# Hybrid retention and GLA layer: the last gates beside the last attention, two heads' branch products in one PSUM sum, half of the output projection in seven products

## The chip, the core and the metric

The kernel runs on one core of one Trainium2 chip. The metric is the device time of one execution in microseconds, and lower is better. A core has a matrix engine (TensorE, PE in the profile; its weight loads are listed as PEld), a vector engine (VectorE, DVE), a scalar engine (ScalarE, ACT), a general one (GpSimd, POOL) and SyncE (SP), which here only issues transfers. Each engine runs its own list of instructions in order and waits on semaphores. Matrix products are summed in PSUM, which VectorE and ScalarE read; everything else lies in SBUF, and the inputs in DRAM.

## The reference

One layer over 512 positions (and 16 meta positions ahead of them) of width 1024, with two branches that a learned gate merges:

```python
u = rms_norm(h, norm_gain)
proj = u @ w_in          # rq, rk, rv, rg, gq, gk, gv, gg, glr, m_ret, m_gla
o_ret = retention_chunked(rope(rq), rope(rk) * RET_QK_DIM ** -0.5, rv)   # 4 heads
o_ret = head_group_norm(o_ret, ret_norm_gain) * silu(rg)                 # 2048 wide
o_gla = gla_chunked(gq, gk, gv, log_a)
o_gla = head_rms_norm(o_gla, gla_norm_gain) * silu(gg)                   # 1024 wide
merged = sigmoid(m_ret) * (o_ret @ w_branch_ret) + sigmoid(m_gla) * (o_gla @ w_branch_gla)
out = rms_norm(h + merged @ w_out, final_norm_gain)                      # meta rows dropped
```

All inputs are float32.

## The kernel before

Float32 accuracy is had from a split: each operand is written as a high part in the fp32r format and a low part, the rest (`split`, line 155: a ScalarE cast for the high part, a VectorE subtraction for the low). A product then takes three matmuls, high by high, high by low and low by high (`mm3`, line 190).

The kernel is one long stream of such products on TensorE, with the other engines' work set beside it. A "dense" generator makes products and a "chain" generator makes a step of attention or of some other dependent work; `weave` (line 206) takes a step of the chain after each step of the dense one. The order in which the program is written is a wish: the framework's planner simulates the engines and puts on each what is ready first, so an instruction written later can stand earlier. `after` (line 160) fixes one instruction behind another on an engine, `pin` and `order` do this for the dense products, and `act` and `vec` for ScalarE and VectorE at the start.

Most projections use `quad` (line 259): a 512-wide block of the result is made from two column blocks and two row halves by seven products (24 matmuls of 256 columns each) instead of eight. For that, sums of weight blocks are needed (`x3`, `x1` and two running sums) and sums of the activations, which are made once at the start (forms S1 to S4 beside A11, A12, A22). With `adds=True` the weight sums x3 and x1 come from accumulating transfers that POOL issues (line 277); with `adds=False` VectorE makes them (lines 330 and 331). Three PSUM tiles a, b and c hold the results, and ScalarE copies one of them aside before the next product is added onto it (`copy`, line 309). Weights come into six buffers ("raw", line 251), their high and low parts into three each. There are two sets of four PSUM banks: `ppt` and `pat` (lines 149 to 153).

The stages in time are: the start (the first projection, GLA's values of pair 0, is fed block by block, lines 512 to 573, with 11 warm-up matmuls ahead of it at line 541; after it the scaled x is made in place at line 580); GLA's two pairs, with their gates; then the four retention heads. Of a head, `ret_qk`, `ret_g` and `ret_v` are quads, `ret_scores` makes the decayed scores, and `ret_attention` (line 1095) has six steps: four blocks of values with a group norm each (VectorE statistics, a power on POOL at line 203, a scaling on ScalarE), and two steps of transposes that write the split head output `oh`, `ol`. `ret_branch` (line 1177) multiplies a head's output by its 512 rows of `w_branch_ret`: 8 tiles of 128 x 512, 12 matmuls each. Heads 0 to 2 copy each tile out on ScalarE and add it to the DRAM buffer `kept2` by an accumulating transfer (`collect`, line 905). GLA's gated result waits in `kept`, also in DRAM.

At the end, `weave(run(ret_branch(2), gates_ret()), every(ret_attention(3), 2))` at line 1203 runs head 2's branch and the second half of the retention gates (the quad `mr1`) beside head 3's attention. `gates_ret` (line 1149) also loads `kept2` into `kr` (line 1164, on POOL behind the last power), multiplies it by the gates and accumulates `kept` onto it (`part`, lines 1156 to 1160). Head 3's branch (line 1221) is merged tile by tile: gate times PSUM (line 1184), plus `kr` (1185), then split into `mh`, `ml`. The output projection is two halves of 512 columns: `proj_b` (line 404) with its four weights in order, and lines 1250 to 1269 with all four weights at hand, a row block of 128 at a time, the last in two halves of 256. `evac_out` (line 1226) adds the residual, sums squares, and, when a row block is whole, scales and stores it.

Of the kernel before, what the change touches and what calls it, by code (L numbers as in the profile page):

```python
# [108 lines left out]
def hybrid_kernel(ctx: ExitStack, tc: tile.TileContext, I, out: bass.AP):  # L109
# [17 lines left out]

    nc.scalar.activation(pad[:, :1], one, AF.Copy, scale=one)
# [130 lines left out]
    def quad(cols, rows, name, evac, meta=None, adds=True, ahead=False, behind=None):  # L259
# [8 lines left out]

        def block(kh, n):
            return w_in[kh * 512:kh * 512 + 512, cols[n]:cols[n] + 256].rearrange("(k p) c -> p k c", p=P)  # L270
# [22 lines left out]
        def product(i, form, w, ps, fresh, ready=None):  # L293
            hi, lo = ready or prepare(i, w)
            for t in range(2):
                col = slice(t * P, (t + 1) * P)
                for kk in range(4):
                    u = [f[form][:, kk, col] if rows else f[form][:, kk, :256] for f in (fh, fl)]
# [105 lines left out]
    def proj_b(src, col, left, name, evac):  # L404

        pss = [ppt(f"{name}_p{t}") for t in range(NTB)]
# [107 lines left out]
    for q in range(4):  # L514
        raw = wraw(f"gv0_{q}_w", (P, 2, 512))
        for s in (slice(0, 1), slice(1, 2)) if q == 0 else (slice(0, 2),):
            k0, n = 2 * q + s.start, s.stop - s.start
            nc.sync.dma_start(u[k0 // 4][:, k0 % 4:k0 % 4 + n], I["xt"][:, k0:k0 + n])
# [21 lines left out]
    for _ in range(11):  # L540
        nc.tensor.matmul(wps, wzero[:, :P], wzero, start=True, stop=True)
# [10 lines left out]
    pss = [ppt(f"gv0_p{t}") for t in range(NTB)]  # L552
    for q in range(4):
        raw = graw[q]
        hi, lo = wsplit([P, 2, 512], f"gv0_{q}")
        for kk in range(2):
            kh, k = divmod(2 * q + kk, 4)
            g = ng[:, 2 * q + kk:2 * q + kk + 1]
            nc.scalar.activation(xh[kh][:, k, :, :HT], u[kh][:, k], AF.Copy, scale=g)
            nc.vector.scalar_tensor_tensor(xl[kh][:, k, :, :HT], u[kh][:, k], g, xh[kh][:, k, :, :HT].bitcast(F32),  # L560
                                           op0=ALU.mult, op1=ALU.subtract)
            split(hi[:, kk, :], lo[:, kk, :], raw[:, kk, :])
# [532 lines left out]
    def ret_attention(h):  # L1095
# [3 lines left out]
        oh = rp.tile([P, 4, T], F32R, tag="oh", name=f"oh{h}")  # L1099
        ol = rp.tile([P, 4, T], F32R, tag="ol", name=f"ol{h}")  # L1100
# [48 lines left out]
    def gates_ret():  # L1149
# [6 lines left out]
        def part(c, s):  # L1156

            k = kr[c][:, :, s]
            after(nc.vector.tensor_mul(k, k, sigr[c][:, :, s]), low[1])
            nc.gpsimd.dma_start(k, kept[:, 2 * c:2 * c + 2, s], accum_op=ALU.add)  # L1160

        for c in range(KD // 2):
            kr[c] = rp.tile([P, 2, T], F32, tag=("sh", "sl", "cs", "dec")[c], name=f"kr{c}")
            after(nc.gpsimd.dma_start(kr[c], kept2[:, 2 * c:2 * c + 2, :]), R["pow"])
            if c < 2:
                pend.append((4 + c, lambda c=c: part(c, slice(0, T))))
        one = sp.tile([P, 1], F32, tag="one", name="sig1")
        pend.append((3, lambda: after(nc.scalar.activation(one, mhalf, AF.Sigmoid), low[0])))

        def evac(n, th, p, q):  # L1170
            s = slice(th * 256, (th + 1) * 256)
            gate(sigr[2 + n][:, :, s], p, q, th, n)
            pend.append((2, lambda: part(2 + n, s)))

        yield from quad((C_MR + 512, C_MR + 768), False, "mr1", evac, adds=False)

    def ret_branch(h):
        def evac(c, ps):
            t = tmp(f"mt{h}{c}")
            if h < 3:  # L1180
                nc.scalar.copy(t, ps)  # L1181
                collect(kept2[:, c, :], t, h == 0)
            else:
                nc.vector.tensor_mul(t, sigr[c // 2][:, c % 2, :], ps)  # L1184
                nc.vector.tensor_add(t, t, kr[c // 2][:, c % 2, :])
                split(mh[c // 2][:, c % 2, :], ml[c // 2][:, c % 2, :], t)

        oh, ol = R["o", h]
        yield from branch(I["w_branch_ret"], h * 512, oh, ol, f"br{h}", evac, pat if h < 2 else ppt)

    for h in range(4):
# [12 lines left out]
    mh, ml = [[cp.tile([P, 4, T], F32R, tag=f"x{n}0", name=f"m{n}0"),  # L1204
               *[cp.tile([P, 2, T], F32R, tag=f"f{n}{i}", name=f"m{n}{i}") for i in (S2, S3)]] for n in "hl"]
    mh, ml = [[m[0][:, :2], m[0][:, 2:], *m[1:]] for m in (mh, ml)]

    def merged(k, t):
        return [m[k // 2][:, k % 2, t * P:(t + 1) * P] for m in (mh, ml)]


    fgb = rp.tile([P, D], F32, tag="sg", name="fgb")
    nc.sync.dma_start(fgb, I["final_norm_gain"].to_broadcast([P, D]))
    hs = [rp.tile([P, NTB, 512], F32, tag="vh", name="hs0"), rp.tile([P, NTB, 512], F32, tag="vl", name="hs1")]

    def residual():
        for half in range(2):
            nc.sync.dma_start(hs[half], I["x"][:, half * 512:(half + 1) * 512].rearrange("(t p) d -> p t d", p=P))
            yield

    weave(ret_branch(3), residual(), skip=3)
# [4 lines left out]
    def evac_out(half):  # L1226
        def f(t, ps, o=0, n=512):
            hh = hs[half][:, t, o:o + n]
# [71 lines left out]
```

## Time and profile before

| | |
|---|---|
| time, median of 3 runs | 781.37 us (781.2 to 782.45) |
| the profiled execution's own time | 781.41 us |
| its span, first to last instruction | 779.6 us |
| granted TensorE clock, mean | 0.998 |
| instructions | 13602 |
| HBM read, written | 98.15 MB, 15.73 MB |

A row of the page's fifth part or of the groups is one kind of instruction: line, engine, operation, out<-in tiles, shape and count, then busy time in us and mean ns, then the idle time before it and who ended it. A row of the timeline or chain begins with the start and the duration in us. A row of the stretches gives the stretch, its length, and for each engine the busy time and in brackets the number of instructions. TensorE is pipelined: a matmul is listed for longer than it holds the engine, so its price is read from the distance between starts.

### The profile page before, as it was taken

How to read it: one execution, taken by the hardware profiler on the slowest of the kernel's cores; microseconds unless marked ns; L12 is line 12 of the kernel's file. 1: busy time of each engine (PE TensorE's matmuls, PEld its weight loads, DVE VectorE, ACT ScalarE, POOL GpSimd, SP SyncE). 2: the span in 40 equal slices, each digit the busy share in tenths (PEclk: the TensorE clock that was granted, in tenths of full speed). 3: DMA queues.
4: the chain of work that ended last, by engine and by line, in shares of the span. 5: the costliest groups of instructions: out<-in, count | busy, mean ns of one | idle time of the engine just before them, and what ended most of it. 6: DMA issues, size and time to landing. Idle time of an engine off the chain costs nothing.

```text
span 779.6 us, 13602 instructions
## 1 busy us (share of the span) xinstructions
PE 767.5 (98%) x5404; PEld 696.3 (89%) x5404; DVE 571.1 (73%) x824; ACT 450.6 (58%) x745; POOL 138.9 (18%) x190
## 2 busy tenths in 40 slices
PE   9999999999999999999999999999999999999896
PEld 6799989999888899999899999989999998898685
DVE  5868788676654679779967688977687988585832
ACT  8889764678564456545656545646455744363422
POOL 2311120101322312100320100330111101321031
PEclk9999999999999999999999999999999999999999
DMA  9862511833249973833693553694465336698102
GB/s 289 264 154 78 111 55 55 190 110 97 79 124 232 238 160 99 189 108 109 201 252 115 134 137 111 170 246 130 124 158 120 110 108 186 120 328 230 55 5 104
DMA packets 92871, 114.76 MB, mean 147 GB/s; under 512 B 5764, under 2 KB 79364, under 8 KB 92552
## 3 DMA queue, kind: packets, MB, share of 16 engines
q1 hardware_dynamic: 73400, 84.27, 34.4%
q0 software_dynamic: 19264, 29.37, 19.7%
q8 instruction: 42, 0.69, 0.4%
q10 hardware_dynamic: 144, 0.26, 0.1%
q14 instruction: 21, 0.17, 0.1%
HBM read 98.15 MB, written 15.73 MB: 146 GB/s over the span
## 4 chain that ended last, share of the span: by engine, by line
PE 86%; DVE 5%; DMA 3%; ACT 3%; issue 2%; POOL 1%; POOLq 0%; DVEq 0%; ACTq 0%
PE rv_b L303 6%; PE rqk_b L303 6%; PE rg_b L303 6%; PE rqk_c L303 3%; PE gv_p L570 3%; PE rg_c L303 3%; PE mg_b L303 3%; PE rv_c L303 3%; PE br_p L191 3%; PE br_p L195 3%; PE br_p L194 3%; PE gg_b L303 2%; PE bg_p L191 2%; PE bg_p L195 2%; PE bg_p L194 2%
## 5 line engine op out<-in xcount | busy, mean ns | idle before, releaser
L191 PE MATMUL br_p<-oh,br_h 128*128 128x512 f32 x128 | 50.6, 395 | 0.0
L195 PE MATMUL br_p<-oh,br_l 128*128 128x512 f32 x128 | 50.6, 395 | 0.0
L194 PE MATMUL br_p<-ol,br_h 128*128 128x512 f32 x128 | 50.5, 395 | 0.0
L156 ACT CAST rv_h<-rv_w 128x1024 fp32r<-128x1024 f32 x24 | 25.3, 1052 | 29.3 <-DVE rv_w L333 10.1
L907 POOL DMA_DIRECT2D kept<-mt x24 | 20.9, 871 | 110.4 <-ACT mt L1181 110.4
L1117 ACT ACTIVATE on<-av,nm,g_r 128x512 f32<-128x512 f32 x16 | 12.5, 778 | 45.4 <-DVE nm L1115 45.4
L156 DVE TENSOR_TENSOR rv_l<-rv_w,rv_h 128x1024 fp32r<-128x1024 f32 x24 | 29.3, 1223 | 8.8 <-ACT rv_h L156 8.8
L156 DVE TENSOR_TENSOR rg_l<-rg_w,rg_h 128x1024 fp32r<-128x1024 f32 x20 | 24.4, 1220 | 7.9 <-ACT rg_h L156 7.9
L191 PE MATMUL wo_p<-wo_h,mh 128*128 128x512 f32 (+1 forms) x72 | 26.9, 374 | 2.5 <-DVE mt L1184 2.5
L195 PEld LDWEIGHTS br_p<-oh,br_l 128*128 128x128 f32 x128 | 24.0, 188 | 5.8
L194 PEld LDWEIGHTS br_p<-ol,br_h 128*128 128x128 f32 x128 | 24.0, 188 | 5.1
L277 POOL DMA_DIRECT2D rqk_x<-in_w_in_dram x8 | 10.5, 1310 | 101.6 <-DMA rqk_x<-in_w_in_dram 40.5
L156 ACT CAST rg_h<-rg_w 128x1024 fp32r<-128x1024 f32 x20 | 21.1, 1053 | 13.0 <-PE br_p L194 5.0
L191 PEld LDWEIGHTS br_p<-oh,br_h 128*128 128x128 f32 x128 | 24.0, 188 | 5.1
L156 DVE TENSOR_TENSOR rqk_l<-rqk_w,rqk_h 128x1024 fp32r<-128x1024 f32 x20 | 24.4, 1220 | 5.4 <-ACT rqk_h L156 5.4
L156 ACT CAST rqk_h<-rqk_w 128x1024 fp32r<-128x1024 f32 x20 | 21.0, 1049 | 12.4 <-DVE rqk_w L333 6.7
L303 PE MATMUL rqk_b<-fh,rqk_h 128*128 128x256 f32 x96 | 27.0, 282 | 0.0
L303 PE MATMUL rg_b<-rg_h,fl 128*128 128x256 f32 x96 | 27.0, 281 | 0.0
L303 PE MATMUL rv_b<-rv_h,fl 128*128 128x256 f32 x96 | 27.0, 281 | 0.0
L303 PE MATMUL rqk_b<-fh,rqk_l 128*128 128x256 f32 x96 | 27.0, 281 | 0.0
L303 PE MATMUL rv_b<-rv_l,fh 128*128 128x256 f32 x96 | 27.0, 281 | 0.0
L303 PE MATMUL rg_b<-rg_l,fh 128*128 128x256 f32 x96 | 26.9, 281 | 0.0
(647 smaller groups left out, 3166.4 us busy)
## 6 DMA issues: line engine op xcount, KB each, us to landing
rv_w<-in_w_in_dram SPq DMA_DIRECT2D x16, 512.0 KB, 4.1
br_w<-in_w_branch_ret_dram SPq DMA_DIRECT2D x16, 512.0 KB, 3.7
rqk_w<-in_w_in_dram SPq DMA_DIRECT2D x12, 512.0 KB, 4.6
rg_w<-in_w_in_dram SPq DMA_DIRECT2D x12, 512.0 KB, 4.6
kept<-mt POOLq DMA_DIRECT2D x24, 256.0 KB, 5.2
bg_w<-in_w_branch_gla_dram SPq DMA_DIRECT2D x8, 512.0 KB, 3.7
mr_w<-in_w_in_dram SPq DMA_DIRECT2D x8, 512.0 KB, 3.5
kept<-gb POOLq DMA_DIRECT2D x16, 256.0 KB, 4.2
```

The source lines that it names most:

```text
L156: return nc.scalar.copy(hi, src), nc.vector.tensor_sub(lo, src, hi.bitcast(F32))
L191: m = nc.tensor.matmul(o, lh, rh, start=first, stop=False)
L194: nc.tensor.matmul(o, lh, rl, start=False, stop=False)
L195: m = nc.tensor.matmul(o, ll, rh, start=False, stop=last)
L277: x = nc.gpsimd.dma_start(t, block(0, 1), accum_op=ALU.add)
L303: m = nc.tensor.matmul(ps[:, t, :], l, r, start=first and j == 0, stop=kk == 3 and j == 2, skip_group_check=not fresh or t == 1)
L570: m = nc.tensor.matmul(pss[t], (al if j == 1 else ah)[t // 2, kh][:, k, c], (lo if j == 2 else hi)[:, kk, :], start=q == kk == j == 0, sto ...
L907: nc.gpsimd.dma_start(dst, t, **({} if first else {"accum_op": ALU.add}))
L1117: nc.scalar.activation(on, ps, AF.Identity, scale=r, bias=nm)
```

## The change

There are five parts.

1. The start. The first x block (k = 0) is loaded from ScalarE's queue, and the small activation that brings the function table is put behind that issue. The loads of the second pair of blocks are single, as those of the first were. There are 10 warm-up matmuls for 11. The first weight's high part is cast on VectorE. Within the first two pairs the order of the three matmuls of a block is changed for the first block. The scalings at line 580 for the first half stand behind the last cast.
2. The gates. `mr1` runs beside head 3's attention alone, with `adds=True`, one attention step per product. `kr` takes other buffers, and its loads are no longer fixed behind the power. Head 3's `oh`, `ol` lie in the buffers of x's first half.
3. The branches. Heads 2 and 3 are multiplied together in `ret_branches`: for each half of the 1024 columns, four PSUM tiles get head 2's products and then head 3's, and are merged once. `part` is called in the first half, for a whole `kr` tile. Head 2 has no copy and no `collect`. The residual and the final gain are loaded in the last two steps.
4. The output projection. Columns 0 to 255 are made plainly (`wo_first`, in the `pat` banks), columns 256 to 767 as a quad of seven products with the merged activations as its forms, and columns 768 to 1023 plainly, a row block at a time. `merged_sums` makes the four sums of merged blocks and splits them, a step after each of the quad's first products.
5. The end. Squares are summed for each 256 columns (`square`), and for the last of them the scaling and addition of the sum is done by ScalarE instead of POOL.

```diff
-    nc.scalar.activation(pad[:, :1], one, AF.Copy, scale=one)
...
-    def quad(cols, rows, name, evac, meta=None, adds=True, ahead=False, behind=None):
+    def quad(cols, rows, name, evac, meta=None, adds=True, ahead=False, behind=None, src=None,
+             forms=None):
+        src, forms = src or w_in, forms or (fh, fl)
...
-        for s in (slice(0, 1), slice(1, 2)) if q == 0 else (slice(0, 2),):
+        for s in (slice(0, 1), slice(1, 2)) if q < 2 else (slice(0, 2),):
             k0, n = 2 * q + s.start, s.stop - s.start
-            nc.sync.dma_start(u[k0 // 4][:, k0 % 4:k0 % 4 + n], I["xt"][:, k0:k0 + n])
+            x = (nc.sync if k0 else nc.scalar).dma_start(u[k0 // 4][:, k0 % 4:k0 % 4 + n], I["xt"][:, k0:k0 + n])
+            if k0 == 0:
+                after(nc.scalar.activation(pad[:, :1], one, AF.Copy, scale=one), x)
...
-    for _ in range(11):
+    for _ in range(10):
...
+            cast = nc.scalar.activation(xh[kh][:, k, :, :HT], u[kh][:, k], AF.Copy, scale=g)
+            casts.append(cast)
+            if k == kh == 0:
+                nc.vector.tensor_copy(hi[:, kk, :], raw[:, kk, :])
+                w = nc.vector.tensor_sub(lo[:, kk, :], raw[:, kk, :], hi[:, kk, :].bitcast(F32))
...
-            steps.sort(key=(lambda x: x[1:]) if q == 0 else (lambda x: x[1]))
+            steps.sort(key=(lambda x: (x[1], -x[2] % 3 if x[1] == 0 else x[2])) if q < 2 else (lambda x: x[1]))
...
             if kh == 1:
                 act(x)
+            else:
+                after(x, casts[-1])
...
-            after(nc.gpsimd.dma_start(kr[c], kept2[:, 2 * c:2 * c + 2, :]), R["pow"])
+            nc.gpsimd.dma_start(kr[c], kept2[:, 2 * c:2 * c + 2, :])
...
-        yield from quad((C_MR + 512, C_MR + 768), False, "mr1", evac, adds=False)
+        yield from quad((C_MR + 512, C_MR + 768), False, "mr1", evac)
+
+    def part(c):
+        after(nc.vector.tensor_mul(kr[c], kr[c], sigr[c]), low[1])
+        nc.gpsimd.dma_start(kr[c], kept[:, 2 * c:2 * c + 2, :], accum_op=ALU.add)
...
+    def ret_branches():
+        for half in range(2):
+            pss = [ppt(f"br_p{c}") for c in range(4)]
+            for h in (2, 3):
+                oh, ol = R["o", h]
+                for q in (2 * half, 2 * half + 1):
...
+                    low[:] = split(hi, lo, raw)
+                    if half == 0:
+                        part(2 * (h - 2) + q)
+                    for cc in range(2):
+                        c = 2 * q + cc
+                        ps = pss[c % 4]
+                        for k in range(4):
+                            mm3(ps, hi[:, k, cc * P:(cc + 1) * P], lo[:, k, cc * P:(cc + 1) * P], oh[:, k], ol[:, k],
+                                h == 2 and k == 0, h == 3 and k == 3, True)
+                        if h == 3:
+                            t = sigr[c // 2][:, c % 2, :]
+                            nc.vector.tensor_mul(t, t, ps)
+                            nc.vector.tensor_add(t, t, kr[c // 2][:, c % 2, :])
+                            split(mh[c // 4][:, c % 4, :], ml[c // 4][:, c % 4, :], t)
+                        yield
...
-    weave(run(ret_branch(2), gates_ret()), every(ret_attention(3), 2))
+    weave(gates_ret(), ret_attention(3))
...
+    def merged_sums():
+        a = [[sigr[2 * kh + j][:, :, th * 256:(th + 1) * 256] for j in range(2)] for th in range(2) for kh in range(2)]
+        a00, a01, a10, a11 = a
+        def parts_of(i, x):
+            for j in range(2):
+                split(mforms[0][i][:, 2 * j:2 * j + 2], mforms[1][i][:, 2 * j:2 * j + 2], x[j])
+        for j in range(2):
+            nc.vector.tensor_sub(a11[j], a11[j], a10[j])
+            nc.vector.tensor_sub(a10[j], a00[j], a10[j])
+        for j in range(2):
+            nc.vector.scalar_tensor_tensor(a00[j], a11[j], -1.0, a00[j], op0=ALU.mult, op1=ALU.subtract)
+        parts_of(S2, a00)
+        yield
+        parts_of(S3, a10)
+        yield
+        parts_of(S1, a11)
+        for j in range(2):
+            nc.vector.scalar_tensor_tensor(a01[j], a00[j], -1.0, a01[j], op0=ALU.mult, op1=ALU.subtract)
+        yield
+        parts_of(S4, a01)
+        yield
...
-    weave(ret_branch(3), residual(), skip=3)
+    weave(ret_branches(), residual(), skip=14)
...
+        if o == 768:
+            nc.scalar.activation(v, ss, AF.Identity, scale=1.0 / D, bias=vs[t])
+        else:
+            nc.gpsimd.tensor_scalar(v, ss, 1.0 / D, vs.get(t, EPS), op0=ALU.mult, op1=ALU.add)
...
-    drain(proj_b(I["w_out"], 0, merged, "wo0", evac_out(0)))
...
+    def wo_first():
+        pss = [pat(f"wo0_p{t}") for t in range(NTB)]
+        for kh in range(2):
+            hi, lo = wo_split(0, kh)
+            for t in range(NTB):
+                for k in range(4):
+                    mm3(pss[t][:, :256], *merged(4 * kh + k, t), hi[:, k], lo[:, k], kh == k == 0, kh == 1 and k == 3,
+                        True)
+                if kh:
+                    add(t, 0, pss[t])
             yield
...
+    def evac_wo(n, th, p, q):
+        d = hs[n][:, 2 * th:2 * th + 2, (256, 0)[n]:(512, 256)[n]]
+        if q is not None:
+            nc.vector.tensor_add(q, p, q)
+            p = q
+        if n == 0:
+            nc.vector.tensor_add(d, d, p)
+        else:
+            nc.vector.scalar_tensor_tensor(d, p, -1.0, d, op0=ALU.mult, op1=ALU.add)
+        for t in (2 * th, 2 * th + 1):
+            square(t, 256 + 256 * n)
+
+    drain(wo_first())
+    weave(quad((256, 512), True, "wo1", evac_wo, src=I["w_out"], forms=mforms), merged_sums())
+    last = [wo_split(768, kh) for kh in range(2)]
+    for t in range(NTB):
+        ps = pat(f"wo2_p{t}")
+        for k in range(KD):
+            hi, lo = last[k // 4]
+            mm3(ps[:, :256], *merged(k, t), hi[:, k % 4], lo[:, k % 4], k == 0, k == KD - 1, True)
+        add(t, 768, ps)
```

More of the change, by code (lines that the diff above doesn't have):

```diff
@@ L297, in product @@
                 for kk in range(4):
-                    u = [f[form][:, kk, col] if rows else f[form][:, kk, :256] for f in (fh, fl)]
+                    u = [f[form][:, kk, col] if rows else f[form][:, kk, :256] for f in forms]
                     v = [f[:, kk, :] if rows else f[:, kk, col] for f in (hi, lo)]
@@ L402, in load_b, with proj_b @@
         loaded[name, q] = raw
-    def proj_b(src, col, left, name, evac):
-        pss = [ppt(f"{name}_p{t}") for t in range(NTB)]
+    def proj_b(src, col, left, name, evac, bank=ppt):
+        pss = [bank(f"{name}_p{t}") for t in range(NTB)]
         for q in range(4):
@@ L552, in hybrid_kernel @@
     pss = [ppt(f"gv0_p{t}") for t in range(NTB)]
+    casts = []
     for q in range(4):
@@ L1098, in ret_attention @@
         vm, sg = R["vm", h], R["sg", h]
-        oh = rp.tile([P, 4, T], F32R, tag="oh", name=f"oh{h}")
-        ol = rp.tile([P, 4, T], F32R, tag="ol", name=f"ol{h}")
+        oh, ol = [(rp if h < 3 else cp).tile([P, 4, T], F32R, tag=f"o{n}" if h < 3 else f"x{n}0", name=f"o{n}{h}")
+                  for n in "hl"]
         R["o", h] = oh, ol
@@ L1249, in hybrid_kernel @@
-    drain(proj_b(I["w_out"], 0, merged, "wo0", evac_out(0)))
-    last = []
-    for q in range(4):
-        load_b(I["w_out"], 512, q, "wo1")
-        raw = loaded.pop(("wo1", q))
-        if q < 2:
-            hi = rp.tile([P, 2, 512], F32R, tag=("qh", "kh")[q], name=f"wo1_{q}_h")
-            lo = rp.tile([P, 2, 512], F32R, tag=("ql", "kl")[q], name=f"wo1_{q}_l")
-        else:
-            hi, lo = wsplit([P, 2, 512], f"wo1_{q}")
-        split(hi, lo, raw)
-        last.append((hi, lo))
-    evac = evac_out(1)
@@ L1262, in hybrid_kernel @@
-    for t in range(NTB):
-        for o, n in ((0, 512),) if t < NTB - 1 else ((0, 256), (256, 256)):
-            ps = ppt(f"wo1_p{t}{o}")
-            for k in range(KD):
-                hi, lo = last[k // 2]
-                mm3(ps[:, :n], *merged(k, t),
-                    hi[:, k % 2, o:o + n], lo[:, k % 2, o:o + n], k == 0, k == KD - 1, True)
-            evac(t, ps, o, n)
+    weave(gates_ret(), ret_attention(3))
+    mh, ml = [[cp.tile([P, 4, T], F32R, tag=f"x{n}1", name=f"m{n}0"),
+               rp.tile([P, 4, T], F32R, tag=("sg", "vl")[n == "l"], name=f"m{n}1")] for n in "hl"]
@@ new lines, in hybrid_kernel @@
+    sums = [[cp.tile([P, 4, 256], F32R, tag=f"f{n}{i}", name=f"ms{n}{i}") for i in range(3, 7)] for n in "hl"]
+    mforms = [[m[0][:, :, :256], m[1][:, :, :256], m[1][:, :, 256:], *x] for m, x in zip((mh, ml), sums)]
+    def merged(k, t):
+        return [m[k // 4][:, k % 4, t * P:(t + 1) * P] for m in (mh, ml)]
+    def merged_sums():
[19 more added lines that the diff above has]
+        yield
@@ new lines, in add, with wo_split @@
+    def add(t, o, ps):
+        hh = hs[o // 512][:, t, o % 512:o % 512 + 256]
+        nc.vector.tensor_add(hh, hh, ps[:, :256])
+        square(t, o)
+    def wo_split(o, kh):
+        raw = wraw(f"wo{o}_w{kh}")
+        nc.sync.dma_start(raw, I["w_out"][kh * 512:kh * 512 + 512, o:o + 256].rearrange("(k p) c -> p k c", p=P))
+        w = wsplit([P, 4, 256], f"wo{o}_{kh}")
+        split(*w, raw)
+        return w
+    def wo_first():
[8 more added lines that the diff above has]
+                    add(t, 0, pss[t])
+            yield
```

98 lines of the change are left out of this document (42 added, 56 removed).

## The prediction

> **What bounds the kernel now.** I read the page's sums first, then the engines by stretch at the end of the span, then TensorE's timeline for its gaps, and last the chain of waits for what ended each gap.
>
> ```profile
> span 779.6 us, 13602 instructions
> PE 767.5 (98%) x5404; PEld 696.3 (89%) x5404; DVE 571.1 (73%) x824; ACT 450.6 (58%) x745; POOL 138.9 (18%) x190
> ```
>
> TensorE is the bound: 767.5 of 779.6 us, so time is won only by taking products away, by closing its gaps, or at the two ends. By stretch (columns: PE, weight loads, DVE, ACT, POOL, clock, DMA share, GB/s):
>
> ```profile
> 580.00:600.00 20.00, 20.00 (x149) 18.98 (x148) 14.04 (x28) 10.32 (x17) 4.32 (x5) 1.00 0.67 152
> 690.00:700.00 10.00, 9.53 (x81) 9.33 (x80) 9.64 (x14) 6.65 (x12) 3.54 (x4) 1.00 1.06 331
> 710.00:720.00 10.00, 10.00 (x45) 8.01 (x44) 2.23 (x5) 1.57 (x2) 0.00 (x0) 1.00 0.82 223
> 720.00:730.00 10.00, 8.01 (x33) 5.54 (x31) 9.91 (x14) 5.28 (x7) 0.00 (x0) 1.00 0.31 107
> 740.00:760.00 20.00, 20.00 (x89) 16.40 (x88) 6.46 (x8) 5.67 (x13) 6.75 (x10) 1.00 0.01 3
> ```
>
> From 710 to 720 VectorE is nearly idle (2.23 of 10 us) and then full (9.91), and there TensorE loses time. The gaps in TensorE's timeline, with the last branch product (724.32) and the last product of all:
>
> ```profile
> 696.41 0.38 PE L303 MATMUL mr_c<-xh,mr_h 128*128 128x256 f32 x1 [0.47 <-ACT mr_x L312]
> ...
> 724.32 0.40 PE L195 MATMUL br_p<-oh,br_l 128*128 128x512 f32 x1
> 724.98 0.47 PE L191 MATMUL wo_p<-wo_h,mh 128*128 128x512 f32 x1 [0.26 <-DVE mt L1184]
> ...
> 727.22 0.50 PE L191 MATMUL wo_p<-wo_h,mh 128*128 128x512 f32 x1 [0.61 <-DVE mt L1184]
> ...
> 730.15 0.50 PE L191 MATMUL wo_p<-wo_h,mh 128*128 128x512 f32 x1 [1.28 <-DVE mt L1184]
> ...
> 732.13 0.50 PE L191 MATMUL wo_p<-wo_h,mh 128*128 128x512 f32 x1 [0.32 <-DVE mt L1184]
> ```
> ```profile
> 772.22 0.28 PE L195 MATMUL wo_p<-wo_h,ml 128*128 128x256 f32 x1
> ```
>
> The chain says why:
>
> ```profile
> 682.39 10.47 DMA kr<-kept
> ...
> 704.63 12.92 DMA wo_w<-in_w_out_dram
> 717.62 1.05 ACT wo_h L156
> 718.66 0.53 ACT mh L156
> ...
> 721.81 0.69 DVE mt L1185
> 722.49 0.75 DVE wo_l L156
> 723.54 0.68 DVE ml L156
> 724.23 0.60 DVE mt L1184
> ```
>
> The DMA engines are full from 690 on (share 1.06): the gate products are loaded and accumulated onto `kept` there, beside the loads of the residual. The output weight lands 12.92 us after its issue; ScalarE, in order, stands at its cast until 717.62; the merged casts (`mh`) stand behind it, VectorE behind them, and the output's four PSUM tiles, which take the banks of the last branch tiles, wait for VectorE's reading of those.
>
> **The change part by part.** The profiled execution took 781.41 us (span 779.6, 1.8 around it), 0.04 above the median of the runs, 781.37.
>
> *Pitch.* A 512-wide product costs 0.232 us (17.85 us for 77, the stretch of the branch tiles below), a 256-wide one 0.1188 (2.85 for 24): two narrow ones cost 0.006 more than one wide.
>
> ```profile
> 700.00:720.00 20.00, 17.85 (x77) 14.44 (x78) 2.03 (x3) 0.00 (x0) 1.00 0.96 244
> ```
> ```profile
> 604.09 2.85 PE rg_a L303 x24
> ```
>
> *Output projection.* Now: 168 wide and 48 narrow products, 168 x 0.232 + 48 x 0.1188 = 44.7 us; the stage takes 47.8 (724.55, when the last branch product has streamed, to 772.34), so the gaps are 3.1. After: 96 narrow for the first 256 columns, 7 x 24 = 168 for the next 512, 96 for the last: 360 x 0.1188 = 42.8. That is -5.0 if no gap stays: 1.9 from products and 3.1 from gaps, since the first tiles now come from the other, free set of banks (`pat`), and kr's traffic is off this place.
>
> [...]
>
> What the seven-product form adds lies on VectorE and ScalarE: 8 adds of 128x512 and 8 splits for the four operand sums, two weight adds, seven weight splits. Prices:
>
> ```profile
> L156 DVE TENSOR_TENSOR wo_l<-wo_w,wo_h 128x1024 fp32r<-128x1024 f32 x8 | 9.7, 1221 | 7.2 <-ACT wo_h L156 7.2
> L156 DVE TENSOR_TENSOR ml<-mt,mh 128x512 fp32r<-128x512 f32 x8 | 5.5, 689 | 8.6 <-ACT mh L156 8.5
> L1185 DVE TENSOR_TENSOR mt<-mt,kr 128x512 f32<-128x512 f32 x8 | 5.5, 686 | 0.1
> L1229 DVE TENSOR_TENSOR hs<-hs,wo_p 128x256 f32<-128x256 f32 x2 | 0.8, 415 | 2.1 <-PE wo_p L195 2.1
> ```
>
> Count from T0, the end of the branch products. TensorE reaches the quad's product 1 at 11.4 us, 2 at 14.3, the first sum product (6) at 17.1, then 7 at 20.0, 5 at 22.8, 4 at 25.7, 3 at 28.5, the last column block at 31.4. VectorE until 17.1: the last merge 2.05, one output split 1.22, four adds 1.7, splits of w11 and w21 2.4, six sums 4.1, their split 1.4, the weight add and its split 2.4: 15.3, so it is ready. Until 20.0 it has 20.6, until 25.7 27.1, until 31.4 32.3: late by at most 1.4 at full durations, and not at all where they overlap by the 0.09 of the chain's rows (0.69 from 721.81, 0.60 from 724.23). So 0 to 1.4; I take 0.7, the middle, as no row decides. If that cover were gone the price is in the second rival. On SP, the residual and the final gain are now loaded in the last two of sixteen branch steps (12 x 0.232 = 2.8 us each), ahead of later output weights; the first add wants them at T0 + 7.1, so 12.7 us after the issue, against the 12.92 of the worst landing above: nothing, or 0.2.
>
> *Branches.* 192 wide products before and after, in two halves of 96; TensorE is unchanged. Gone: eight ScalarE copies and eight accumulating transfers of head 2. The four gate multiplies and accumulates move into the first half: the first is wanted by the first merge, 48 + 12 products x 0.232 = 13.9 us later, and a 1.2 us multiply plus the 10.47 us landing above is 11.7. VectorE while head 3 runs in a half (11.1 us) has four merges of 2.05 and up to four operations of 1.22: 13.1, so 2.0 late at worst in the first half, which head 2's light turn absorbs. PSUM: half two's first bank is free after c=0's multiply, three tiles (8.4 us) earlier.
>
> *Gates beside attention.* Head 3's attention gets one step per product, as head 2's had from 580 on, where TensorE never stops (20.00 of 20). The weights are added by accumulating transfers, which takes 2 x 1.22 from VectorE. Today's gap at 696.41 (0.47, and 0.2 of refill) waits for a ScalarE copy: -0.7 when gone. What could come: the four kr loads have no fixed place behind POOL's powers any more; two wait for the score tiles, and behind them on POOL would stand the powers that attention's normalisation waits for. Bounds 0 to 1.5 (four issues of 0.6, less the cover of a product):
>
> ```profile
> L1164 POOL DMA_DIRECT2D kr<-kept x4 | 2.5, 637 | 8.4 <-DMA kept<-mt 8.3
> L203 POOL TENSOR_TENSOR g_r<-g_v,mhalf 128x1 f32<-128x1 f32 x4 | 2.2, 562 | 7.2 <-DVE g_v L202 7.2
> ```
>
> I take +0.5 for gates and branches together.
>
> *Start.*
>
> ```profile
> 0.73 1.28 ACT L128 ACT_TABLE_LOAD   x1 [0.73 <-PEq L1290]
> 0.73 0.39 SPq L512 DMA_DIRECT2D ng<-in_norm_gain_dram  x1
> ...
> 1.17 0.42 SPq L518 DMA_DIRECT2D u<-in_xt_dram  x1
> 1.18 0.13 PEld L541 LDWEIGHTS <-warm 128*128 128x128 bf16 x2 [1.18 <-DVE warm L538]
> 1.18 4.59 PE L541 MATMUL warm_p<-warm 128*128 128x512 bf16 x11 [1.18 <-DVE warm L538]
> ...
> 4.22 0.73 ACT L559 ACTIVATE xh<-u,ng 128x528 fp32r<-128x528 f32 x1 [1.90 <-DMA u<-in_xt_dram]
> ...
> 5.54 0.76 PEld L570 LDWEIGHTS gv_p<-gv_h,xh 128*128 128x128 f32 x4 [0.39 <-ACT gv_h L156]
> ...
> 8.52 0.75 PEld L570 LDWEIGHTS gv_p<-gv_h,xh 128*128 128x128 f32 x4 [0.37 <-ACT gv_h L156]
> ...
> 12.06 0.19 PEld L570 LDWEIGHTS gv_p<-gv_l,xh 128*128 128x128 f32 x1 [0.47 <-DVE gv_l L156]
> ```
>
> On ScalarE's queue the first x block is issued 0.44 sooner, at 0.73, ahead of the table load (1.28 us, over well before it lands at 3.8), and the first weight, 0.47 sooner on SP, is cast on VectorE beside x. The tenth warm-up product ends 0.42 before the eleventh did, so the first real one gains 0.2 to 0.45. The two later waits (0.37, 0.47) shrink with the finer loads: 0 to 0.6. I take -0.5. Moved behind the casts are four scalings of 0.73 (2.9 us of ScalarE), which then delay its queue; TensorE has 20 us of first products as cover, and without it up to 2.9 would show.
>
> *End.* The last sum of squares is scaled on ScalarE instead of POOL (0.27 and the hop): -0.15.
>
> Sum: -0.5 - 0.7 + 0.5 - 5.0 + 0.7 - 0.15 = -5.2; 781.41 - 5.2 = 776.2 us.
>
> **The rivals.** First, half exposed: VectorE's new work is not slipped into its gaps fully. Against the written order it would cost, as in the next rival, 11.8; half is 5.9, so 776.2 - 0.7 + 5.9 = 781.4, no change. For it: 9.91 of 10 busy at 720. Against: 6.46 of 20 from 740.
>
> Second, slower: VectorE runs the output stage in the order written. The four adds to the residual, which wait for TensorE, stand ahead of w11's split, and the sums ahead of w21's. Product 1 then starts 1.6 late, product 2 another 3.9, product 6 another 4.0, product 7 another 2.3: 11.8 in all, 787.3 us. It decides for slower from 7.4 us of stall on. Against: the chain shows `wo_l` at 722.49 between merges, though it is written after all of them, so the planner does move what is ready.
>
> Third, weight loads set the pace of narrow products (0.19 us a load, as at 12.06): 360 x 0.19 = 68.4 for 42.8, so 776.2 + 25.6 = 801.8. What speaks against it is the row of 24 narrow products in 2.85 us. [...]
>
> That the change doesn't do what it says I rule out: 24 narrow products and the copies of head 2 are not issued.
>
> **How the numbers follow.** Forecast 0.74, half exposed 0.08, written order 0.09, weight loads 0.01; 0.08 I leave to the forecast with a stall of 2 to 4 us, at 778 to 780. A measurement tells 0.2% (1.6 us), so the bound of faster is 779.8. Faster 0.82, same 0.08, slower 0.10. Without any new stall the sum is 775.0, with the start's best case 774.5; the range goes a little below, to 773.8, and up to 780.2, which leaves about 2 in 10 out. The forecast's own range is 774.5 to 778.
>
> **What would show it.** Right: no gap over 0.3 at the first `wo0` product, a stage of 43 to 44 us from there to the last product, 360 narrow products, no release by `L1184`, kr landing off the chain, the gap before `mr_c` gone, first product near 5.2. Wrong: gaps before the quad's sum products with VectorE as the releaser and VectorE full there; transposes of attention waiting for POOL; a later first product; a DMA share of 1 under the output weights.

## The result, and the profile after

The changed kernel takes 774.45 us (median of 4 runs, 774.07 to 775.05), beside 781.38 for the kernel before on the same chip: a ratio of 0.9909, 95% interval 0.9893 to 0.9925. The forecast was 776.2 in a range of 773.8 to 780.2. The time lies just under the forecast's own range, 774.5 to 778. The gain is 6.9 us where the sum had 5.2, and the terms do not all stand as the sum had them. (The profiled execution took 775.05 us, so the table below adds up to 6.4.)

The page's sums, and the stretches that answer to those shown of before (columns: PE, weight loads, DVE, ACT, POOL, clock, DMA share, GB/s):

```profile
span 773.3 us, 13943 instructions
PE 762.9 (99%) x5547; PEld 703.7 (91%) x5547; DVE 588.6 (76%) x848; ACT 457.6 (59%) x768; POOL 141.5 (18%) x191
```
```profile
690.00:700.00 10.00, 10.00 (x45) 8.26 (x44) 7.93 (x11) 3.13 (x5) 0.00 (x0) 1.00 1.06 279
710.00:720.00 10.00, 10.00 (x46) 8.29 (x45) 6.90 (x10) 3.35 (x4) 1.29 (x1) 1.00 0.93 264
720.00:730.00 10.00, 10.00 (x80) 9.73 (x78) 10.00 (x17) 6.66 (x12) 0.04 (x1) 1.00 0.30 76
740.00:760.00 20.00, 19.89 (x166) 19.55 (x165) 15.08 (x19) 11.97 (x30) 7.66 (x13) 1.00 0.01 3
```

TensorE no longer stops from 690 to 730 (it had 9.53 and 8.01 of 10 in two of those stretches). VectorE, nearly idle at 710 before (2.23 of 10), now works 6.90 there; at 720 it is as full as it was (10.00), but no longer stops TensorE. TensorE's timeline, at the first and last product of the two heads' branches, the first of the output, the one stall in the output stage (with the start of the product behind it, 747.86), and the last product:

```profile
677.97 0.39 PE L189 MATMUL br_p<-oh,br_h 128*128 128x512 f32 x1
...
721.31 0.39 PE L193 MATMUL br_p<-oh,br_l 128*128 128x512 f32 x1
721.53 0.28 PE L189 MATMUL wo_p<-wo_h,mh 128*128 128x256 f32 x1
...
744.29 0.28 PE L304 MATMUL wo_c<-wo_h,msl 128*128 128x256 f32 x1
744.68 0.38 PE L304 MATMUL wo_b<-wo_h,msh 128*128 128x256 f32 x1
...
747.86 0.28 PE L304 MATMUL wo_c<-wo_h,mh 128*128 128x256 f32 x1
...
764.86 0.28 PE L193 MATMUL wo_p<-wo_h,ml 128*128 128x256 f32 x1
```

The output stage lasts 43.4 us (721.53 to 764.97, when the last product has streamed). The chain of waits of the same execution says what the stall is:

```profile
742.53 0.69 DVE hs L1341
743.24 0.91 ACT fsq L1292 x4
744.15 0.48 ACT wo_x L313
744.68 3.34 PE wo_b L304 x24
748.02 2.83 PE wo_c L304 x24
```
```profile
743.24 0.42 ACT L1292 ACTIVATE fsq<-hs 128x256 f32<-128x256 f32 x1 [1.37 <-DVE hs L1341]
```

The fifth of the quad's seven products needs bank b, whose content ScalarE must first copy aside (`wo_x`). The copy stands behind two sums of squares on ScalarE (two instructions each), and ScalarE has sat idle for 1.37 us because these wait for VectorE's addition. TensorE waits 0.27 us and starts again slowly: from 744.29 to 747.86 it takes 3.57 us for 25 matmuls that take 2.97 at 0.1188, so the stall costs 0.6 us.

Where the time went, from the starts of the same products in both timelines (us; minus is gained):

| stretch | before | after | gain |
|---|---|---|---|
| last of GLA's first values | 28.14 | 28.03 | -0.1 |
| from there to the last values of head 3 | 620.4 | 619.4 | -1.0 |
| from there to the last branch product | 75.8 | 73.8 | -2.0 |
| output stage | 47.8 | 43.4 | -4.4 |
| from there to the end of the span | 7.3 | 8.3 | +1.0 |

The second row holds products that the change leaves alone, and yet they take 1.0 us less; of the third row's 2.0 the sum knew 0.7. In these two traces the start gave less than predicted, and the end got longer. Most of the experiments are about these.

### The profile page after: what moved, and what is told of

Read it like the earlier page. It is cut to its first block, busy times and chain, and to the rows that moved or that the text cites. A ratio compares the mean times of both kernels' runs of the same rounds, so it can differ in the third digit from the quotient of the medians.

```text
span 773.3 us, 13943 instructions
## 1 busy us (share of the span) xinstructions
PE 762.9 (99%) x5547; PEld 703.7 (91%) x5547; DVE 588.6 (76%) x848; ACT 457.6 (59%) x768; POOL 141.5 (18%) x191
## 4 chain that ended last, share of the span: by engine, by line
PE 88%; DVE 6%; ACT 3%; issue 2%; POOL 1%; POOLq 0%; DVEq 0%; ACTq 0%
PE rqk_b L304 6%; PE rv_b L304 6%; PE rg_b L304 6%; PE br_p L193 3%; PE br_p L189 3%; PE br_p L192 3%; PE gv_p L582 3%; PE mr_b L304 3%; PE rqk_c L304 3%; PE mg_b L304 3%; PE rg_c L304 3%; PE rv_c L304 3%; PE gg_b L304 2%; PE bg_p L193 2%; PE bg_p L189 2%; PE bg_p L192 2%
## 5 line engine op out<-in xcount | busy, mean ns | idle before, releaser
L154 ACT CAST br_h<-br_w 128x1024 fp32r<-128x1024 f32 x16 | 16.8, 1051 | 23.9 <-PE br_p L192 9.5
L304 PE MATMUL rqk_b<-fl,rqk_h 128*128 128x256 f32 x96 | 27.0, 282 | 0.0
L304 PE MATMUL rv_b<-rv_h,fh 128*128 128x256 f32 x96 | 27.0, 281 | 0.0
```

What stands on the lines that cost most here:

```text
L154: return nc.scalar.copy(hi, src), nc.vector.tensor_sub(lo, src, hi.bitcast(F32))
L304: m = nc.tensor.matmul(ps[:, t, :], l, r, start=first and j == 0, stop=kk == 3 and j == 2, skip_group_check=not fresh or t == 1)
```

## The experiments

Each was timed beside the kernel before. Behind each median stand the ratio to that kernel and, in brackets, its 95% interval.

**The start alone**, in the kernel before (`b_start`: part 1 of the change, nothing else).

> The kernel before with the new start alone. My step said 0.5 us faster (780.9). The profile after shows the first product 0.47 earlier but the clock granted in full only at 6.7 us instead of 5.4, and the end of the first projection only 0.11 earlier. If the clock's opening follows the shorter warm-up: 781.3, within 0.2 of before. If it is a matter of the execution's phase: 780.6 to 780.9 in most executions, and the profile shows full clock before 5.6 us.

781.4 us, 0.9999 [0.999, 1.0007]: no gain is seen, though the interval, from 0.8 us faster to 0.5 slower, does not rule out the 0.5. TensorE's first products, of before, of after and of this run:

```profile
1.18 4.59 PE L541 MATMUL warm_p<-warm 128*128 128x512 bf16 x11 [1.18 <-DVE warm L538]
5.54 1.20 PE L570 MATMUL gv_p<-gv_h,xh 128*128 128x512 f32 x4
```
```profile
1.18 4.45 PE L545 MATMUL warm_p<-warm 128*128 128x512 bf16 x10 [1.18 <-DVE warm L542]
5.07 2.06 PE L582 MATMUL gv_p<-gv_h,xh 128*128 128x512 f32 x4
```
```profile
5.57 1.24 PE L579 MATMUL gv_p<-gv_h,xh 128*128 128x512 f32 x4
```

In the changed kernel's trace the first product starts 0.47 us sooner, as predicted, but the first four take 2.06 us instead of 1.20. In this run's trace they take 1.24, but the first of them starts no sooner than before. The weight's cast, now on VectorE, is what differs there (this run, then after):

```profile
4.26 1.17 DVE L564 CAST gv_h<-gv_w 128x512 fp32r<-128x512 f32 x1 [3.14 <-DMA gv_w<-in_w_in_dram]
```
```profile
4.23 0.61 DVE L567 CAST gv_h<-gv_w 128x512 fp32r<-128x512 f32 x1 [3.11 <-DMA gv_w<-in_w_in_dram]
```

Ten traces have the new start. In seven the cast takes 1.02 to 1.27 us and the first product starts at 5.57 to 5.61; in three (after, `a_dve12`, `a_dma5`) it takes 0.57 to 0.61 and the first product starts at 4.99 to 5.07. In the four traces with the old start it starts at 5.43 to 5.67. Why the same cast takes twice as long in most traces is open. The last of GLA's first values comes at 27.64 us on average with the new start and at 27.86 with the old, so a gain of 0.2 is what the traces suggest.

The pace of the first products is the other matter. With the same start in `a_dma5` (below) they take this:

```profile
1.18 4.16 PE L545 MATMUL warm_p<-warm 128*128 128x512 bf16 x10 [1.18 <-DVE warm L542]
4.99 1.28 PE L582 MATMUL gv_p<-gv_h,xh 128*128 128x512 f32 x4
```

So 2.06 against 1.28 is not the code: TensorE reaches its full pace at a point that varies by execution. The clock record that each trace keeps begins, at full clock, between 3.9 and 6.8 us from the start of the span: at 5.36 in before, 6.75 in after, 5.71 in `b_start`, 4.91 in `a_dma5`. In after, products start 0.43 us apart just ahead of it and 0.23 behind it. What the earlier data win can be lost to that. What sets the point is not shown: the last three have the same ten warm-up products, so their number alone does not set it. The rows of stretches print a clock of 1.00 for the time ahead of the record and do not show it.

**The banks alone**, in the kernel before (`b_bank`).

```diff
-        pss = [ppt(f"{name}_p{t}") for t in range(NTB)]
+        pss = [pat(f"{name}_p{t}") for t in range(NTB)]
```

> The kernel before with the first half of the output projection in the other four PSUM banks, nothing else moved. My step: the 3.1 us of gaps at the first output products stand for the wait on the banks of the last branch tiles, so they shrink to 0 to 0.8 us and the time falls by 2.3 to 3.1 us, to about 778.7. Rival: the merge itself is late, because its casts stand behind the late output weight on ScalarE; the gaps only move to the products that need the last merged tiles, and the time falls by less than 1 us.

777.36 us, 0.995 [0.9938, 0.9962]. One word gives 4.1 us. Last branch product and first output product:

```profile
723.88 0.39 PE L195 MATMUL br_p<-oh,br_l 128*128 128x512 f32 x1
724.11 0.39 PE L191 MATMUL wo_p<-wo_h,mh 128*128 128x512 f32 x1
```

No gap is left, though the loads, the casts and VectorE's burst stay as they were: TensorE had waited for the banks. The stage is 44.15 us for the same products, so the gaps had weighed 3.6 and not 3.1; the rest of the 4.1 is, in this trace, a first projection that ended 0.4 sooner. The rival, that the merge itself is late and the gaps only move, falls.

**The place of the buffers.** The branch products are faster after: 191 distances from 677.97 to 721.31 are 0.2269 us each, where before 95 distances took 0.2334:

```profile
702.15 0.40 PE L191 MATMUL br_p<-oh,br_h 128*128 128x512 f32 x1
```

(to 724.32, shown in the prediction). GLA's branch, which the change does not touch, also went from 0.2333 to 0.2286. What did change there is the pool of small tiles: `one` has one buffer instead of five and the `fv` tiles eight instead of ten, six of 32 bytes in all by count, so every buffer placed after them lies 192 bytes lower. In `b_shift64` the kernel before gets 64 bytes more ahead of them, and in `a_shift64` the changed kernel does; each engine's instructions stay the same.

```diff
-    pad = sp.tile([P, 8], F32, name="pad", bufs=1)
+    pad = sp.tile([P, 24], F32, name="pad", bufs=1)
```

> The kernel before with one small tile made 64 bytes longer, so that every buffer laid out after it (the heads' outputs among them) starts 64 bytes later; the lists of instructions are the same. In the profile after, a 512-wide branch product takes 0.227 to 0.229 us where it took 0.2333 before, and the only thing that differs for heads 0 and 1 is this start, 64 instead of 0 modulo 128. Theory 'place in memory': the pitch follows the start, so 192 + 384 wide products gain 0.0042 each, and the time falls by 2.0 to 2.6 us to about 779.1, with 0.229 a product in the branches. Rival 'chip or run': the pitch is a matter of the execution, and the time stays within 0.3 us of 781.4.

780.26 us, 0.9987 [0.9978, 0.9996]: a gain of 1.2 us, short of the expected 2.0 to 2.6 but beyond the rival's 0.3. Groups of GLA's branch products, before and then with 64 bytes more (duration of one in ns: least/median/most, first and last start):

```profile
L191 PE MATMUL bg_p<-goh,bg_h x64: 388/395/586, 188.9 to 261.9; 128*128 128x512 f32 x64
```
```profile
L191 PE MATMUL bg_p<-goh,bg_h x64: 387/389/579, 188.7 to 261.1; 128*128 128x512 f32 x64
```

The stretch is 72.4 us instead of 73.0 with nothing moved but addresses. From GLA's first values to head 3's last, 619.5 us for 620.4: the whole of what the second row of the table shows. In the branches of heads 2 and 3 a product takes 0.2274 us for 0.2333. The branches end 1.5 us sooner (722.84 for 724.32), 0.3 of it from a sooner first projection, but the span is only 1.1 shorter. Part of what the place gives is lost where TensorE now waits for the same banks already in the last branch, and longer at the first output product:

```profile
720.19 0.50 PE L191 MATMUL br_p<-oh,br_h 128*128 128x512 f32 x1 [0.61 <-DVE mt L1184]
724.00 0.47 PE L191 MATMUL wo_p<-wo_h,mh 128*128 128x512 f32 x1 [0.77 <-DVE mt L1184]
```

> The kernel after with the same 64 bytes, which bring the starts back to 0 modulo 128 for the GLA outputs and the outputs of heads 0 to 2 (head 3's lie elsewhere and stay at 64). Theory 'place in memory': slower by 1.3 to 2.2 us, about 776.2, with the branches of heads 0 and 1 at 0.233 us a product. Rival 'chip or run': no change, 774.4 within 0.4 us.

775.14 us, 0.9919 [0.9907, 0.9931], between the theory's 776.2 and the rival's 774.4 and not told apart from the changed kernel's 0.9909. The products stay at 0.2293 us in the branches of heads 0 and 1 and 0.2283 in those of heads 2 and 3. So the reading that a start on a multiple of 128 bytes is the slow one falls. What the runs show is that before's placing is slow, that 192 less or 64 more (equal modulo 256) is fast, and that 128 less is nearly as fast (`a_oldout` below, which by count also lies 128 lower, has 0.2295 in GLA's branch and 0.2283 in those of heads 2 and 3). Which operand matters, and why, is open.

**Both small edits** (`b_bank64`: the bank's word and the 64 bytes, in the kernel before).

> The kernel before with two edits of one number or word: its first four output tiles in the attention's banks, and 64 more bytes ahead of the later buffers. If the two gains add (the pitch of the branch products falls from 0.2333 to 0.229 us, 1.5 us up to the end of the branches, and with free banks nothing at the first output product takes it back): 775.7 to 776.2 us. If the shorter branches come back as new gaps in the output stage, as with the 64 bytes alone: 776.8 us or more.

776.54 us, 0.9936 [0.9922, 0.9949]: between the two expectations, nearer to the one where they add. In its trace they do: the branches end at 722.50, the output stage has no gap and lasts 44.0 us, and the span is 774.0, 1.5 under that with the bank alone; by the ratios it is 1.1 us, and those intervals overlap. Two edits of a word and a number thus give 0.64% of the change's 0.91%.

**The seven products**, taken out of the changed kernel (`a_plain`).

```diff
-    weave(quad((256, 512), True, "wo1", evac_wo, src=I["w_out"], forms=mforms), merged_sums())
-    last = [wo_split(768, kh) for kh in range(2)]
-    for t in range(NTB):
-        ps = pat(f"wo2_p{t}")
...
+    for o in (256, 512, 768):
+        last = [wo_split(o, kh) for kh in range(2)]
+        for t in range(NTB):
+            ps = pat(f"wo{o}_p{t}")
```

> The changed kernel with columns 256 to 767 made by the same plain narrow products as columns 0 to 255: no seven products, no sums of merged parts or of weights. 384 narrow products in the output stage instead of 360. If the seven products earn what the sum gave them: 24 products of 0.1185 us come back (+2.8) and the 0.74 us stall in front of the last of the seven goes, so the stage lasts 45.5 us instead of 43.44 and the time is about 776.5 us. Rival, that the 15 extra VectorE instructions cost as much elsewhere (in the branch stage before, or in the end) as the products save: 774.0 to 775.2 us.

776.36 us, 0.9934 [0.9921, 0.9946], where the sum of products and stall gave 776.5. The stage is 45.6 us, 2.2 longer, with no stall. So the seven products earn about 2 us against narrow plain ones.

**The old output form behind the new branches** (`a_oldout`: parts 1 to 3 of the change, then `proj_b` in the `pat` banks and the 512-wide second half).

> The changed kernel up to the branch stage, with the output projection of the kernel before (512 wide products, last row block in two halves), its first four tiles in the attention's banks. If the free banks were what the output stage gained, the stage lasts 44.2 us (44.15 with the banks alone in the kernel before), the last stores are 5.5 us apart again and the end takes 7.3 us instead of 8.3: 774.0 to 775.0 us, no slower than the changed kernel. If the seven products earn what the sum gave them (1.9 us): 776 us or more.

775.62 us, 0.9921 [0.9908, 0.9935], between the expected 774.0 to 775.0 and the rival's 776. The last branch product and the last product of its trace:

```profile
721.76 0.39 PE L193 MATMUL br_p<-oh,br_l 128*128 128x512 f32 x1
...
766.10 0.28 PE L193 MATMUL wo_p<-wo_h,ml 128*128 128x256 f32 x1
```

The stage is 44.2 us, 0.8 over the changed kernel's, and the end 0.7 shorter. Against the old form in free banks, then, the new one earns 0.8 in the stage and gives 0.7 back at the end. The edit moves more than the output form, though: this kernel has the old ten `fv` tiles, so its buffers lie 128 bytes lower and not 192, and from GLA's first values to the last branch product it takes 0.6 us more (693.9 for 693.3). That is most of the difference in time, and the intervals do not tell the two kernels apart.

**The cover of the sums** (`a_hold`: the first sum of merged parts stands on VectorE behind the last addition of the first output columns).

```diff
+            x = nc.vector.tensor_sub(a11[j], a11[j], a10[j])
+            if j == 0:
+                after(x, held[0])
```

> The changed kernel with the first sum of merged parts held on VectorE behind the last addition of the first output columns (end at 734.83 in its trace), so that the sums run in the order in which they are written instead of from 719.97 on. About 7.1 us of VectorE time of the sums lay before 734.83. The prediction's rival of the written order gave +11.1 us, that is 785.5 us. Theory now, that what VectorE does not do for the sums it does for the merges and splits beside them, which then come earlier, but that PE waits for the sums: +5 to +7 us, 779.5 to 781.5 us, with the new gap in front of the first product that takes a sum. If the cover is wide: under 776 us.

777.48 us, 0.9949 [0.9937, 0.9962]: some 3 us slower than the changed kernel, so the sums' early place does matter. It is not the price of the written order, because the edit holds only one of the two halves of the sums (j = 0). The other half still stands early on VectorE, ahead of the last addition (L1315):

```profile
725.92 0.69 DVE L1256 TENSOR_TENSOR sigr<-sigr,sigr 128x512 f32<-128x512 f32 x1
...
733.20 0.41 DVE L1315 TENSOR_TENSOR hs<-hs,wo_p 128x256 f32<-128x256 f32 x1
733.53 1.17 DVE L1256 TENSOR_TENSOR sigr<-sigr,sigr 128x512 f32<-128x512 f32 x1
```

Of the ten operations of the sums that lay ahead of that addition in the changed kernel, six still do, and the weight splits were not held at all. So neither the prediction's rival (11.8 us) nor the 5 to 7 us of the theory was tested as written. TensorE's two new gaps, the stretches, and the clock behind the gaps:

```profile
739.43 0.39 PE L304 MATMUL wo_b<-wo_h,msh 128*128 128x256 f32 x1 [0.96 <-ACT msh L154]
741.19 0.38 PE L304 MATMUL wo_b<-wo_h,msl 128*128 128x256 f32 x1 [1.25 <-DVE msl L154]
```
```profile
720.00:730.00 10.00, 10.00 (x80) 9.77 (x80) 9.25 (x14) 4.93 (x7) 0.00 (x0) 1.00 0.29 84
730.00:740.00 10.00, 8.97 (x74) 8.56 (x72) 10.00 (x15) 6.43 (x15) 6.90 (x8) 1.00 0.16 55
742.00:746.00 4.00, 4.00 (x23) 4.00 (x22) 3.81 (x5) 1.61 (x7) 1.80 (x2) 0.57 0.00 0
```

VectorE is busy 9.25 of 10 from 720 on without the held half: merges and weight splits that would have come later take its place, so part of the held work is exchanged and not lost. The output stage of this trace is 3.6 us longer. The two gaps cost 2.7, and 1.5 comes from something else: the granted clock falls to 0.50 from 742.36 to 745.77, and 16 matmuls there start 0.213 us apart instead of 0.119 (the 0.6 us stall of the changed kernel is gone). The profiled execution took 778.34 us; whether the others, from 776.79 on, had this drop is not on record.

**The long end.** In the changed kernel the transfers in the last 6 us are these (GB/s in 40 slices from 767.0 to 773.3, and the queues):

```profile
GB/s 390 169 0 0 0 0 0 0 0 0 13 325 403 377 390 390 377 416 325 274 26 0 13 13 26 13 0 0 0 0 0 0 0 0 0 0 0 52 0 0
q14 instruction: 2, 0.02, 0.9%
out_dram<-hs ACTq DMA_DIRECT2D x1, 256.0 KB, 3.7
```

The last two stores run at about 400 GB/s, and then a few packets trickle in for another 0.9 us, behind an 8 KB packet of instructions that the trace has at 769.8 us. That stores 2.85 us apart crowd each other, which seemed likely, falls with `a_plain`: it has the same spacing, and its last store lands as soon after its issue as before's (2.7). To find whose fetch it is, twelve fills of one number were written ahead of the last attention, on VectorE (`a_dve12`) or on GpSimd (`a_pool12`). The planner puts them at the start of the kernel (from 1.07 us on VectorE), ahead of every later fetch of that engine.

```diff
+    for _ in range(12):
+        nc.vector.memset(pad[:, 2:3], 0.0)
     weave(gates_ret(), ret_attention(3))
```

> The changed kernel with twelve fills of one number on VectorE ahead of the last attention, so that every later fetch of VectorE's instructions comes twelve instructions earlier. If the 8 KB fetch that falls into the last stores of the changed kernel (769.8 us) is VectorE's, it moves in front of the last stores, the last one lands 2.7 us after its issue instead of 3.7, the end is 7.4 to 7.8 us instead of 8.4 and the time 773.5 to 773.9 us. If it is another engine's: fetch at the same place, end 8.4 us, 774.5 us.

> The same twelve fills on GpSimd instead. If the fetch at 769.8 us is GpSimd's, it moves in front of the last stores: landing 2.7 us after issue, end 7.4 to 7.8 us, time 773.5 to 773.9 us. If it is another engine's: fetch at the same place, end 8.4 us, 774.5 us.

774.19 us, 0.9898 [0.9883, 0.9912], and 774.65 us, 0.9907 [0.9891, 0.9924]. The first misses the expected 773.5 to 773.9, and the times alone don't tell the two apart; the traces do. With the fills on VectorE (40 slices from 766.5 to 771.6):

```profile
GB/s 113 0 0 0 0 0 0 0 0 0 0 0 337 369 402 369 402 369 402 386 386 386 274 33 0 0 0 0 0 0 0 0 0 0 0 0 0 64 0 0
out_dram<-hs ACTq DMA_DIRECT2D x1, 256.0 KB, 2.8
```

and with them on GpSimd (from 766.9 to 773.1):

```profile
GB/s 383 132 0 0 0 0 0 0 0 0 13 330 396 396 383 370 344 436 357 304 40 0 13 13 26 13 0 0 0 0 0 0 0 0 0 0 0 53 0 0
out_dram<-hs ACTq DMA_DIRECT2D x1, 256.0 KB, 3.7
```

It is VectorE's fetch: moved, it leaves the stores alone, the last lands after 2.8 us and the end is 0.9 shorter. That the changed kernel reaches this fetch fits its 24 more instructions on VectorE (848 for 824); why the fetch lies just there is not shown. The packets are 16 KB on one instruction queue (43 packets, 0.70 MB on the page) and 8 KB on the other (23 packets, 0.19 MB), where this fetch lies.

The other part of the end is SP's list of final waits, one for each transfer semaphore, some 0.07 us each in the trace. The last two stores stand second and third in the changed kernel's list, so that five waits come after them (771.62 to 772.37, with a pause of 0.4 in the middle); before, they stand near its end (778.15 to 778.30). Five small loads on SP turn the semaphores round (`a_dma5`).

```diff
     last = [wo_split(768, kh) for kh in range(2)]
+    for i in range(5):
+        nc.sync.dma_start(pad[:, 2 + i:3 + i], I["xt"][:, 0, 0, i:i + 1])
```

> The changed kernel with five loads of 128 single numbers on SP's queue behind the loads of the last weights; SP waits for nothing there. The end of the changed kernel is 8.4 us from the start of the last product, in three traces alike, against 7.4 before. In it the two last stores are seen at 6.8 us, 3.7 us after their issue, and SP's list of final waits still takes 0.8 us, because their semaphores stand second and third in it; in the kernel before the stores land 2.7 us after issue and stand near the end of the list (0.2 us). Five more transfers move them to the end of the list: end 7.8 us, time about 773.9 us. If it is also SP's own fetch of instructions (an 8 KB packet of the instruction queue at 769.8 us, in the middle of the last stores) that makes the stores late, the end is 6.9 us and the time about 773.0. If the end hangs on something else: 774.5 us, end 8.4.

774.06 us, 0.9897 [0.9882, 0.9912]. The list now ends 0.2 us after the stores are seen, not 0.8, and the end (here from the start of the last product, 8.4 us in the changed kernel) is 0.7 shorter, as the first part of the expectation said; VectorE's fetch is still there and the stores are late. Both edits together (`a_end`):

> The changed kernel with both edits, the twelve fills on VectorE and the five small loads on SP. If the two parts of the long end are independent (VectorE's fetch of instructions in the last stores, 0.95 us; the place of the last two stores in SP's list of final waits, 0.7 us), the end takes 6.7 to 6.8 us instead of 8.4, less than the 7.4 of the kernel before, and the time is about 1.6 us under the changed kernel's: 772.8 to 773.2 us, ratio to the kernel before about 0.989. If they overlap: end 7.4 us or more, 773.7 us or more.

773.57 us, 0.9896 [0.988, 0.9913]. The end is 7.4 us, 1.0 less than the changed kernel's and not 1.6. The stores land 2.9 us after issue, but SP goes on 0.5 us later still. Another 8 KB instruction packet lies there, at 769.9; that it is SP's own, moved by the five loads, is argued and not shown. The median is the lowest of all, but its interval overlaps the changed kernel's.

## Why the prediction was right, and where it was not

*Output projection, the largest term: right in size, and mostly for the reason given.* Predicted 42.8 us plus a stall of 0.7, measured 43.4. `b_bank` confirms that the gaps were the banks'. The split was off by half a microsecond both ways: I priced the wide products at 0.232, the pitch of the branch stage, but in the output they take 0.229 (44.15 us in `b_bank` less 48 x 0.1188, over 168). So fewer products are worth 1.4 before the stall and the banks 3.6. What is left to the seven products and their stall against the old form, 0.8 in the stage, is little for 24 instructions more on VectorE.

*The new stall, 0 to 1.4, taken as 0.7: measured 0.6.* It stands before a sum product as counted, but ScalarE's squares and copy end it, which the count of VectorE left out. That the size agrees is in part luck.

*Gates and branches.* The gap at `mr_c` is gone (-0.7), as predicted. The +0.5 for powers behind the kr loads and for merges did not come.

*The start, -0.5: not confirmed.* The two traces give 0.1, the traces of both starts 0.2 on average, and the interval of `b_start` decides nothing within half a microsecond. The data come sooner, but the step took the weight's cast on VectorE as hidden, where in seven of ten traces it lasts 1.0 to 1.3 us and holds the first product, and it took it that the first products run at the same pace in every execution.

*The end, -0.15: wrong, +1.0.* The operation that the step priced gave what it said: the last stores are issued 3.0 us after the start of the last product, 3.2 before. The step left the stores as they were, but they land 1.0 later (VectorE's fetch), and the list of waits behind them takes 0.6 more. The steps behind the list take 0.4 less (0.9 for 1.3), for a reason that is open.

*Left out altogether: about -2.2 from the place of the buffers*, 1.0 up to head 3's values (0.9 in `b_shift64`) and 192 x (0.2334 - 0.2269) = 1.2 in the last branches, where `b_shift64` has 0.2274 with the old code. "TensorE is unchanged" was the step that failed; the number of products was unchanged, the addresses were not.

*The rivals.* The written order did not come: the chain's `wo_l` between the merges was a true sign of the planner. Its price of 11.8 stays open: holding half of the sums alone costs 3.0. Half exposed (5.9) did not come either, with a stall of 0.6. Weight loads do not set the pace: 24 narrow products take 2.83 us.

That the time fell into the range is in part luck: a gain that the sum did not know (2.2) and a loss of 0.5 that did not come outweighed the errors at the two ends (0.4 and 1.15).

## What to carry to other kernels

When several loads, casts and merges are late together, ask first what the waiting product itself needs: here it was a bank, and one word gave more than half of what a change of five parts did. Before a gain is put down to an edit, compare stretches that the edit leaves alone: a few bytes in a pool of small tiles moved them by 1 to 2 us. Price a product's pitch from the stage in which it stands (the same shape took 0.2334 us in before's branches and 0.229 in the output of `b_bank`), and the last microseconds from the stores and final waits, not from the operations alone.

## What the runs showed of the hardware

- The pitch of the same 512-wide products depends on where the buffers lie: in GLA's and the first two heads' branches 0.233 us in one place, 0.2283 to 0.2295 when everything lies 64 bytes higher or 192 or 128 lower.
- VectorE's fetch of its own instructions, an 8 KB packet of the instruction queue at 769.8 us in the changed kernel, can land in the last stores: the last landed 3.7 us after its issue, and 2.8 with twelve more instructions on VectorE (`a_dve12`), where the end was 0.9 shorter.
- SP's final waits cost about 0.07 us each behind the last store: 0.8 us in all with a pause of 0.4 in the middle, or 0.2 where the last store's semaphore stands near the end of the list.
- TensorE's first four products took 1.20, 2.06 and 1.28 us in three executions, the last two with the same start, and the record of the full clock began between 3.9 and 6.8 us in fourteen traces, so a start tuned by less than a microsecond can't be read from one profile.
- The granted clock can fall to half inside a kernel: in `a_hold` for 3.4 us, with two gaps of about 1 us between products ahead of it, and products then take 0.213 us instead of 0.119. Before's trace has gaps of up to 1.28 us and no such drop, so what brings it is open.
- The same 128x512 cast on VectorE took 0.57 to 0.61 us in three traces and 1.02 to 1.27 in seven; why is open.
